# Decays of a state-space mixer: products with a 0/1 tile against loads from a DRAM tile with a maximum on VectorE

## The chip, the cores and the metric

The kernel runs on one core of one Trainium2 chip. The metric is the device time in microseconds (us) of one execution. TensorE (PE in the rows) multiplies, VectorE (DVE) and ScalarE (ACT) work elementwise, GpSimd (POOL) does small elementwise work, and SyncE (SP) starts nearly all loads. Every engine takes its own instructions strictly in the order in which they were written for it, so an instruction that waits holds up all that stand behind it on that engine.

## What is computed

One layer of a hybrid decoder: two token mixers, their merge, an MLP, a gated embedding and norms, for 512 tokens of 1024 channels. The change lies in one of the mixers, Mamba-2 SSD, in the factor `l_dec`:

```
def ssd_mixer(z, xbc, dt_raw, w_conv, b_conv, dt_bias, a_log, d_skip, out_norm):
    ...                                   # G=4 groups, J=8 heads each, P=64, N=128, chunks of L=128, nc=4
    dt = jax.nn.softplus(dt_raw.astype(f32) + dt_bias.astype(f32))
    a_head = -jnp.exp(a_log.astype(f32)).reshape(G, J)
    ...
    a_cs = jnp.cumsum(dtc * a_head, axis=2)
    Xdt = X * dtc[..., None]
    seg = a_cs[:, :, :, None] - a_cs[:, :, None]
    causal = jnp.tril(jnp.ones((L, L), dtype=bool))[:, :, None, None]
    l_dec = jnp.exp(jnp.where(causal, seg, -jnp.inf))
    scores = jnp.einsum('bclgn,bcsgn->bclsg', Cc, Bc)
    y_diag = jnp.einsum('bclsgj,bcsgjp->bclgjp', scores[..., None] * l_dec, Xdt)
    ...
```

For each of 32 heads and 4 chunks `l_dec` is a 128 x 128 matrix: `exp(a_cs[l] - a_cs[s])` for l >= s. Position s lies on the partitions, l along the free axis, so the row `a_cs[l]` of a head has to be spread over all 128 partitions first. The kernel holds `-a_cs` (it grows along a chunk, and is never negative).

## The kernel before

Products of fp32 matrices are made of three products of rounded parts (a high part and a rest): `mm3`, or the like in `proj_b`. Weights come by SP into two `raw` buffers (line 154), ScalarE rounds them to `whi` (line 164), VectorE makes the rest `wlo` (line 165), each in four buffers, and TensorE takes both (lines 169 to 171 for `proj_a` with results `pa`, 249 to 251 for `proj_b` with results `pb`). The results lie in four PSUM buffers `mm`; small results (`yd`, `yo`, `st`, `bc`, `ot`, ...) lie in four others, `sm`.

The SSD mixer goes group by group. For a group g: `ssd_proj` makes x, B and C by products with the input, with a convolution of four taps on VectorE (`acc`, line 549) and transposes; `ssd_z` makes the gate `sz`; `ssd_pre` makes the scores `scm` and the decays L; `ssd_core` goes over the four chunks, `ssd_gate` gates, normalizes and transposes (`ot`), and `ssd_branch` multiplies with the output weights of the group before. In `ssd_core` a chunk c takes: L times `scm` on VectorE (line 615), `xdt` (617), eight small products `yd` (624), the state's product `yo` for c > 0 (621), the state's update `st` (632) with `S` on VectorE (641), and additions to `Xg` (647, 651) and the gate (660). The product `yo` of chunk c + 1 needs `S` of chunk c.

The decays of a group come in `ssd_pre`: the `-a_cs` of all heads lies as two rounded parts in rows 0 to 63 of the tile `ncsT`, and rows 64 to 127 hold 2^100 at the triangle's forbidden places. A 0/1 tile `sel` picks a head's two rows (GpSimd writes it anew for each group, line 591) and adds the forbidden rows to it: two products a head, one for each half of the 128 positions, spread the sum over the partitions in PSUM (`bc`, line 600), and four `exp` on ScalarE (line 602), one a chunk, write L from it with the own `a_cs[s]` as bias `qt`. There are four L buffers, one a chunk.

Before this, once, a block works out `dt` and `-a_cs` (the tile `dt_s`, named s2) for all heads on VectorE and ScalarE with rows of 32 partitions, and transposes four such rows of results, collected in `dt_Q`, by the product `psq` to `qt`.

The order on each engine comes from a scheduler that simulates the timeline while the program is built; code blocks can be moved ahead in its priorities (`ahead`). So a change in one place moves instructions in others too.

Of the kernel before, what the change touches and what calls it, by code (L numbers as in the profile page):

```python
# [23 lines left out]
HPG = 8  # L24
# [14 lines left out]
def f32(ap):  # L39
    return ap.bitcast(F32)  # L40
# [3 lines left out]
def tile_hybrid_block(  # L44
# [21 lines left out]
    nc = tc.nc  # L66
    V, S, G, TE = nc.vector, nc.scalar, nc.gpsimd, nc.tensor

    cp = ctx.enter_context(tc.tile_pool(name="cp", bufs=1))
# [11 lines left out]
    def sm_ps(name):  # L81
        return psm.tile([P, T], F32, tag="sm", name=name, bufs=4)


    ident = cp.tile([P, P], F32, name="ident")
# [7 lines left out]
        out=cmask, in_=cmask, pattern=[[1, P]], compare_op=ALU.is_ge, fill=0.0,  # L93
# [7 lines left out]
        base=0, channel_multiplier=-1,  # L101
    )
    G.memset(gmask[:64, 64:], 0.0)
    sel64 = cp.tile([64, 32], R, name="sel64")
    V.tensor_copy(sel64[0:32, :], ident[0:32, 0:32])
    V.tensor_copy(sel64[32:64, :], ident[32:64, 32:64])
    prm = cp.tile([P, 232], F32, name="prm")
    dsk = cp.tile([P, 32], F32, name="dsk")

# [384 lines left out]
    wgt = dts.tile([48, 512], F32, name="wgt")  # L494
    nc.sync.dma_start(wgt[32:48, :], w_gla_gate)
    qt = dts.tile([P, NT, P], F32, name="qt")
    ncsT = dts.tile([P, T], R, name="ncsT")
    cdb = dts.tile([P, NT, 32], F32, name="cdb")


    sx = ExitStack()
    sp = sx.enter_context(tc.tile_pool(name="sp", bufs=1, reuse_waits="tile"))

    sel = sp.tile([P, 2, HPG, P], R, name="sel")
    if True:
        pick = sp.tile([P, 2, P], F32, tag="S", name="pick", bufs=2)
        G.memset(pick, 0.0)  # L510
        for v in range(2):

            G.affine_select(
                out=pick[:, v, :], in_=pick[:, v, :], pattern=[[1, P]], compare_op=ALU.not_equal, fill=1.0,
                base=64 - 64 * v, channel_multiplier=-1,
            )

        G.memset(pick[64:65, 0, :64], 0.0)
        G.memset(pick[64:65, 0, 64:], 1.0)
        G.memset(pick[64:65, 1, :], 0.0)  # L520
        G.tensor_copy(sel[64:], pick[64:].unsqueeze(2).to_broadcast([64, 2, HPG, P]))


    def heads(ap, c0, g):

# [50 lines left out]
    def ssd_pre(g):  # L576
        Xg, BT, CT = st[g]["X"], st[g]["BT"], st[g]["CT"]
        ps = sm_ps(f"bt{g}")
        for c in range(NT):
            TE.transpose(ps[:, c * P : (c + 1) * P], BT[:, c * P : (c + 1) * P], ident)  # L580
        Bt = sp.tile([P, NT, P], F32, tag="Bt", name=f"Btok{g}", bufs=1)
        S.copy(Bt, ps.rearrange("p (c n) -> p c n", c=NT))
        ps = sm_ps(f"sc{g}")
        for c in range(NT):
            cc = slice(c * P, (c + 1) * P)
            TE.matmul(ps[:, cc], lhsT=BT[:, cc], rhs=CT[:, cc], start=True, stop=True)
        sc = sp.tile([P, NT, P], F32, tag="sc", name=f"scm{g}", bufs=1)
        V.tensor_tensor(
            sc, ps.rearrange("p (c l) -> p c l", c=NT), cmask.unsqueeze(1).to_broadcast([P, NT, P]), op=ALU.mult
        )  # L590
        G.tensor_copy(
            sel[:64], sel64[:, 8 * g : 8 * g + 8].unsqueeze(1).unsqueeze(3).to_broadcast([64, 2, HPG, P])
        )
        Ls = [sp.tile([P, HPG, P], F32, tag="L", name=f"L{g}_{c}", bufs=4) for c in range(NT)]
        for j in range(HPG):
            h = 8 * g + j
            pb = sm_ps(f"bc{h}").rearrange("p (c v l) -> p c v l", c=NT, v=2)
            nv = ncsT.rearrange("p (c v l) -> p c v l", c=NT, v=2)
            for v in range(2):
                TE.matmul(pb[:, :, v, :], lhsT=sel[:, v, j, :], rhs=nv[:, :, v, :], start=True, stop=True)  # L600
            for c in range(NT):
                S.activation(
                    Ls[c][:, j, :].rearrange("p (v l) -> p v l", v=2), pb[:, c], AF.Exp, scale=-1.0,
                    bias=qt[:, c, 32 + h : 33 + h],
                )
        st[g].update(Bt=Bt, Ls=Ls, sc=sc)

# [87 lines left out]
    if True:  # L695
# [9 lines left out]
        def tl(tag, name, rows=32):  # L705
# [5 lines left out]
        smask = tl("S", "smask")  # L711
        G.memset(smask, 1.0)
        G.memset(smask.rearrange("p (c l) -> p c l", c=NT)[:, :, 0:1], 0.0)

        far = sp.tile([P, 64], F32, tag="S", name="far", bufs=2)
        G.memset(far, 2.0**100)
        G.affine_select(
            out=far, in_=far, pattern=[[-1, 64]], compare_op=ALU.is_ge, fill=0.0, base=-65, channel_multiplier=1,
        )
        G.memset(far[64:65, :], 2.0**100)  # L720
        G.tensor_copy(
            ncsT[64:, :].rearrange("p (c l) -> p c l", l=64), far[64:, :].unsqueeze(1).to_broadcast([64, 8, 64])
        )
        ae = cp.tile([32, 1], F32, name="ae")
        S.activation(ae, alog, AF.Exp)
        V.tensor_scalar(out=xr, in0=ps[:32, :], scalar1=dtb, scalar2=None, op0=ALU.add)
# [17 lines left out]
        V.tensor_scalar(out=s1, in0=xr, scalar1=ae, scalar2=None, op0=ALU.mult)  # L744
        V.tensor_tensor_scan(out=s2, data0=smask, data1=s1, initial=0.0, op0=ALU.mult, op1=ALU.add)
        S.copy(Q[32:64, :], s2)
        S.copy(ncsT[0:32, :], s2)
        V.tensor_tensor(ab, s2, f32(ncsT[0:32, :]), op=ALU.subtract)
        S.copy(ncsT[32:64, :], ab)
        S.activation(Q[64:96, :], s2, AF.Exp, scale=-1.0)  # L750
        s2v = s2.rearrange("p (c l) -> p c l", c=NT)
        V.tensor_tensor(
# [488 lines left out]
```

## Time and profile before

| | us |
|---|---|
| median of 3 runs | 1181.87 |
| lowest, highest | 1176.79, 1185.32 |
| the profiled execution, its own time | 1176.31 |
| its span, first to last instruction | 1174.6 |
| TensorE busy | 1152.0 |
| VectorE busy | 684.4 |
| ScalarE busy | 519.6 |
| GpSimd busy | 154.7 |

Times in the rows are us from the start of the span. The SSD mixer takes the stretch up to about 390 us. Busy time of TensorE counts matmuls that overlap: the time from one start to the next is what one costs. "Idle before" is what an engine sat without work before an instruction, and the name after the arrow is what it waited for. The SP queue's own rows show the transfers it starts, not their landing.

### The profile page before, as it was taken

The page shows a single profiled execution, that of the slowest core. Times are in us where ns is not written, and L with a number is a line of the kernel's source. Part 1 is how long each engine was busy: PE and PEld are TensorE (multiplying, and loading weights), DVE is VectorE, ACT ScalarE, POOL GpSimd, SP SyncE. Part 2 cuts the span into 40 slices and gives each one's busy share as a digit, 9 for nine tenths or more (in the row PEclk, how much of TensorE's full clock was granted, in tenths as well). Part 3 has the DMA queues.
Part 4 walks back from the last instruction along what each step waited for, and adds up shares of the span by engine and source line. Part 5 has one row for each costly group of instructions (what it writes and reads, how often), then busy time and mean ns, then how long its engine had stood idle before and what let it go on. Part 6 is the DMA issues. An engine that isn't in the chain of part 4 may idle for free.

```text
span 1174.6 us, 14039 instructions
## 1 busy us (share of the span) xinstructions
PE 1152.0 (98%) x5540; PEld 955.2 (81%) x5540; DVE 684.4 (58%) x901; ACT 519.6 (44%) x846; POOL 154.7 (13%) x142
## 2 busy tenths in 40 slices
PE   6999999999999999999999999999999999999997
PEld 5887887888887678888888888898888888888786
DVE  6766747767557547244234334665566755766865
ACT  4566483572482217442433232444334443344553
POOL 6003114032013000000021110000021000201212
PEclk9999999999999999999999999999999999999999
DMA  7332122222322143322224332743426452445221
GB/s 209 108 90 79 48 73 72 72 74 72 107 72 74 36 136 119 104 72 72 72 72 126 82 98 72 204 138 95 121 72 177 116 161 84 114 132 122 90 90 72
DMA packets 150177, 117.39 MB, mean 100 GB/s; under 512 B 5456, under 2 KB 124880, under 8 KB 150112
## 3 DMA queue, kind: packets, MB, share of 16 engines
q1 hardware_dynamic: 146048, 107.59, 31.5%
q0 software_dynamic: 2912, 5.77, 2.9%
q10 hardware_dynamic: 1152, 3.15, 0.7%
q8 instruction: 43, 0.70, 0.3%
q14 instruction: 22, 0.18, 0.0%
HBM read 114.40 MB, written 2.10 MB: 99 GB/s over the span
## 4 chain that ended last, share of the span: by engine, by line
PE 94%; DVE 2%; ACT 1%; DMA 1%; issue 1%; SPq 1%; POOL 0%; POOLq 0%; ACTq 0%; DVEq 0%
PE pa L170 18%; PE pa L169 18%; PE pa L171 18%; PE pb L249 7%; PE pb L250 7%; PE pb L251 7%; PE yd L624 2%; PE sX L349 2%; PE sX L348 2%; PE sX L350 2%; PE st L632 1%; PE yo L621 1%; PE sZ L349 1%; PE sZ L350 1%; PE sZ L348 1%; DMA raw<-in_w_in_dram 1%
## 5 line engine op out<-in xcount | busy, mean ns | idle before, releaser
L165 DVE TENSOR_TENSOR wlo<-raw,whi 128x1024 fp32r<-128x1024 f32 (+1 forms) x208 | 261.1, 1262 | 253.4 <-ACT whi L164 253.1
L164 ACT CAST whi<-raw 128x1024 fp32r<-128x1024 f32 (+1 forms) x209 | 216.5, 1039 | 356.5 <-PE pa L170 225.1
L169 PE MATMUL pa<-h1h,whi 128*128 128x512 f32 (+1 forms) x416 | 160.0, 385 | 0.5 <-ACT h1h L419 0.4
L171 PE MATMUL pa<-h1h,wlo 128*128 128x512 f32 (+1 forms) x416 | 157.6, 379 | 0.0
L170 PE MATMUL pa<-h1l,whi 128*128 128x512 f32 (+1 forms) x416 | 156.8, 377 | 0.1
L170 PE MATMUL pa<-h2l,whi 128*128 128x512 f32 (+1 forms) x384 | 142.7, 372 | 0.0
L169 PE MATMUL pa<-h2h,whi 128*128 128x512 f32 (+1 forms) x384 | 142.4, 372 | 0.0
L171 PE MATMUL pa<-h2h,wlo 128*128 128x512 f32 (+1 forms) x384 | 142.2, 372 | 0.0
L249 PE MATMUL pb<-whi,h1h 128*128 128x512 f32 x256 | 99.8, 394 | 0.8 <-DVE accb L684 0.8
L250 PE MATMUL pb<-wlo,h1h 128*128 128x512 f32 x256 | 99.9, 390 | 0.0
L251 PE MATMUL pb<-whi,h1l 128*128 128x512 f32 x256 | 99.5, 392 | 0.0
L169 PEld LDWEIGHTS pa<-h1h,whi 128*128 128x128 f32 x416 | 79.5, 191 | 15.2 <-ACT h1h L419 0.8
L170 PEld LDWEIGHTS pa<-h1l,whi 128*128 128x128 f32 x416 | 79.4, 191 | 14.3 <-issue 0.7
L171 PEld LDWEIGHTS pa<-h1h,wlo 128*128 128x128 f32 x416 | 79.2, 190 | 13.8 <-issue 0.2
L170 PEld LDWEIGHTS pa<-h2l,whi 128*128 128x128 f32 x384 | 72.4, 189 | 12.5
L171 PEld LDWEIGHTS pa<-h2h,wlo 128*128 128x128 f32 x384 | 72.3, 189 | 12.3
L169 PEld LDWEIGHTS pa<-h2h,whi 128*128 128x128 f32 x384 | 72.2, 189 | 12.4
L249 PEld LDWEIGHTS pb<-whi,h1h 128*128 128x128 f32 x256 | 48.1, 188 | 10.5 <-DVE accb L684 1.2
L251 PEld LDWEIGHTS pb<-whi,h1l 128*128 128x128 f32 x256 | 48.1, 188 | 9.7
L250 PEld LDWEIGHTS pb<-wlo,h1h 128*128 128x128 f32 x256 | 48.1, 188 | 9.3
L549 DVE SCALAR_TENSOR_TENSOR acc<-pa,prm,acc 128x511 f32<-128x511 f32 (+2 forms) x72 | 52.6, 742 | 2.9 <-ACT acc L547 2.0
L170 PE MATMUL pa<-obl,whi 128*128 128x512 f32 x128 | 52.0, 406 | 0.0
(380 smaller groups left out, 1981.7 us busy)
## 6 DMA issues: line engine op xcount, KB each, us to landing
raw<-in_w_in_dram SPq DMA_DIRECT2D x48, 512.0 KB, 5.1
raw<-in_w_ffn_up_dram SPq DMA_DIRECT2D x44, 512.0 KB, 5.2
raw<-in_w_in_dram SPq DMA_DIRECT2D x16, 1024.0 KB, 5.1
raw<-in_w_ffn_down_dram SPq DMA_DIRECT2D x10, 1024.0 KB, 5.3
raw<-in_w_branch_b_dram SPq DMA_DIRECT2D x32, 256.0 KB, 3.8
raw<-in_w_branch_a_dram SPq DMA_DIRECT2D x8, 512.0 KB, 4.8
raw<-in_w_out_dram SPq DMA_DIRECT2D x4, 1024.0 KB, 4.9
raw<-in_w_ffn_down_dram POOLq DMA_DIRECT2D x4, 1024.0 KB, 8.7
```

What stands on the lines that cost most here:

```text
L164: S.copy(hi, raw)
L165: eng.tensor_tensor(lo, raw, f32(hi), op=ALU.subtract)
L169: TE.matmul(ps, lhsT=lh, rhs=rh, start=first, stop=False)
L170: TE.matmul(ps, lhsT=lh, rhs=rl, start=False, stop=False)
L171: TE.matmul(ps, lhsT=ll, rhs=rh, start=False, stop=last)
L249: TE.matmul(pss[t], lhsT=a, rhs=hi[:, kk, :], start=first, stop=False)
L250: TE.matmul(pss[t], lhsT=a, rhs=lo[:, kk, :], start=False, stop=False)
L251: TE.matmul(pss[t], lhsT=b, rhs=hi[:, kk, :], start=False, stop=last)
L348: TE.matmul(ps, lhsT=a_h, rhs=hi[:, k % 2, :], start=new and k == 0, stop=False, skip_group_check=True)
L349: TE.matmul(ps, lhsT=a_h, rhs=lo[:, k % 2, :], start=False, stop=False, skip_group_check=True)
L350: TE.matmul(ps, lhsT=a_l, rhs=hi[:, k % 2, :], start=False, stop=k == kh - 1, skip_group_check=True)
L549: V.scalar_tensor_tensor(out=acc[:, s:], in0=ps[:, : T - s], scalar=cw[:, ct, 3 - s : 4 - s], in1=acc[:, s:], op0=ALU.mult, op1=ALU.add,)
```

## The change

The products `bc`, the tiles `sel`, `sel64`, `pick`, `far` and `ncsT` and all that fills them are gone. In their place `-a_cs` is written to a tile in DRAM, `ncsd`, by four transfers from ScalarE's queue, one a chunk. For each group and chunk SP loads the 8 heads' rows (8 x 128 numbers, 4 KB in one piece) into all 128 partitions of the L buffer. VectorE replaces each value by the maximum of it and the own value of the partition (so that forbidden places get exp(0) = 1, which `scm` then zeroes), and the `exp` of ScalarE works in place, eight a chunk, now chunk by chunk.

```diff
-    sel64 = cp.tile([64, 32], R, name="sel64")
-    V.tensor_copy(sel64[0:32, :], ident[0:32, 0:32])
-    V.tensor_copy(sel64[32:64, :], ident[32:64, 32:64])
...
-    ncsT = dts.tile([P, T], R, name="ncsT")
+
+    dram = ctx.enter_context(tc.tile_pool(name="dram", bufs=1, space=bass.MemoryType.DRAM))
+    ncsd = dram.tile([NT, 32, P], F32, name="ncsd")
...
-    sel = sp.tile([P, 2, HPG, P], R, name="sel")
...
-        G.tensor_copy(sel[64:], pick[64:].unsqueeze(2).to_broadcast([64, 2, HPG, P]))
...
-        G.tensor_copy(
-            sel[:64], sel64[:, 8 * g : 8 * g + 8].unsqueeze(1).unsqueeze(3).to_broadcast([64, 2, HPG, P])
-        )
+
         Ls = [sp.tile([P, HPG, P], F32, tag="L", name=f"L{g}_{c}", bufs=4) for c in range(NT)]
-        for j in range(HPG):
-            h = 8 * g + j
-            pb = sm_ps(f"bc{h}").rearrange("p (c v l) -> p c v l", c=NT, v=2)
-            nv = ncsT.rearrange("p (c v l) -> p c v l", c=NT, v=2)
-            for v in range(2):
-                TE.matmul(pb[:, :, v, :], lhsT=sel[:, v, j, :], rhs=nv[:, :, v, :], start=True, stop=True)
-            for c in range(NT):
+        for c in range(NT):
+            src = ncsd[c : c + 1, 8 * g : 8 * g + 8, :].rearrange("c h l -> c (h l)").to_broadcast([P, HPG * P])
+            nc.sync.dma_start(Ls[c].rearrange("p h l -> p (h l)"), src)
+            own = qt[:, c, 32 + 8 * g : 40 + 8 * g].unsqueeze(2).to_broadcast([P, HPG, P])
+            V.tensor_tensor(Ls[c], Ls[c], own, op=ALU.max)
+            for j in range(HPG):
+                h = 8 * g + j
                 S.activation(
-                    Ls[c][:, j, :].rearrange("p (v l) -> p v l", v=2), pb[:, c], AF.Exp, scale=-1.0,
-                    bias=qt[:, c, 32 + h : 33 + h],
+                    Ls[c][:, j, :], Ls[c][:, j, :], AF.Exp, scale=-1.0, bias=qt[:, c, 32 + h : 33 + h],
                 )
...
-        S.copy(ncsT[0:32, :], s2)
-        V.tensor_tensor(ab, s2, f32(ncsT[0:32, :]), op=ALU.subtract)
-        S.copy(ncsT[32:64, :], ab)
+        for c in range(NT):
+            nc.scalar.dma_start(ncsd[c], s2[:, c * P : (c + 1) * P])
```

The order moves with it. SP, while group 1 is in `ssd_core`: the names `raw` are weights (of group 2's input products and gate), `L_0` to `L_3` the decays of the next group. Before:

```order
L154 DMA raw_1762<-in_w_in_dram 128x8x128 [waits DMAHW6_49,DMAHW1_49,DMAHW7_49,DMAHW0_49,DVE_49]
L154 DMA raw_1762<-in_w_in_dram 128x8x128
L154 DMA raw_1968<-in_w_in_dram 128x8x128 [waits DMAHW3_49,DMAHW2_49,DVE_49]
L154 DMA raw_1968<-in_w_in_dram 128x8x128
L154 DMA raw_2152<-in_w_in_dram 128x4x512 [waits DMAHW5_49,DMAHW4_49,DVE_49]
L154 DMA raw_2162<-in_w_in_dram 128x4x512 [waits DMAHW7_49,DMAHW6_49,DVE_49]
```

With the change, SP at the same place:

```order
L151 DMA raw_1899<-in_w_in_dram 128x8x128 [waits DMAHW7_49,DMAHW6_49,DVE_49]
L151 DMA raw_1899<-in_w_in_dram 128x8x128
L574 DMA L_0_1855<-ncsd 128x1024 [waits PE_49]
L574 DMA L_1_1856<-ncsd 128x1024 [waits DMAHW5_49,PE_49]
L574 DMA L_2_1857<-ncsd 128x1024 [waits PE_49]
L151 DMA raw_2083<-in_w_in_dram 128x4x512 [waits DMAHW1_49,DMAHW0_49,DVE_49]
L574 DMA L_3_1858<-ncsd 128x1024 [waits PE_49]
L151 DMA raw_2093<-in_w_in_dram 128x4x512 [waits DMAHW3_49,DMAHW2_49,DVE_49]
```

SP now waits for TensorE too: a load of L takes the buffer that the `yd` products of the same chunk, one group earlier, have read, and three such loads stand ahead of the gate's weights.

VectorE in the same stretch, from the first chunk's `yd` of group 1 to the update of the state. Before:

```order
L647 TENSOR_TENSOR Xg_962<-Xg_962,yd_0_1332 128x512
L617 TENSOR_TENSOR xdt_2_1376<-Xg_962,qt 128x512
L660 TENSOR_TENSOR Xg_962<-Xg_962,sz_0_1420 128x512
L650 TENSOR_TENSOR yt_1_1372<-yo_1_1352,qt 128x512
L165 TENSOR_TENSOR wlo_1807<-raw_1762,whi_1806 128x1024
L647 TENSOR_TENSOR Xg_962<-Xg_962,yd_1_1354 128x512
L617 TENSOR_TENSOR xdt_3_1402<-Xg_962,qt 128x512
L651 TENSOR_TENSOR Xg_962<-Xg_962,yt_1_1372 128x512
L641 TENSOR_TENSOR S_1_1367<-S_1_1367,st_1_1365 128x512
```

With the change, VectorE from the same instruction on:

```order
L623 TENSOR_TENSOR Xg_927<-Xg_927,yd_0_1280 128x512
L593 TENSOR_TENSOR xdt_2_1324<-Xg_927,qt 128x512
L636 TENSOR_TENSOR Xg_927<-Xg_927,sz_0_1368 128x512
L576 TENSOR_TENSOR L_0_1855<-L_0_1855,qt 128x1024
L162 TENSOR_TENSOR wlo_1714<-raw_1710,whi_1713 128x1024
L626 TENSOR_TENSOR yt_1_1320<-yo_1_1300,qt 128x512
L623 TENSOR_TENSOR Xg_927<-Xg_927,yd_1_1302 128x512
L593 TENSOR_TENSOR xdt_3_1350<-Xg_927,qt 128x512
L627 TENSOR_TENSOR Xg_927<-Xg_927,yt_1_1320 128x512
L617 TENSOR_TENSOR S_1_1315<-S_1_1315,st_1_1313 128x512
```

The maximum of group 2's first chunk stands three instructions behind the addition of the `yd` that frees its buffer, and the weights' rests, the additions and the state's update stand behind it. It is so for all four chunks, and for the groups 0 to 2 alike.

ScalarE in the block that works out `-a_cs` (`dt_s_532` before and `dt_s_518` now is s2), up to the first gate `sz_0`. Before:

```order
L746 COPY dt_Q<-dt_s_532 32x512
L747 CAST ncsT<-dt_s_532 32x512
L750 ACT_TABLE_LOAD
L750 ACTIVATE dt_Q<-dt_s_532 32x512
L756 ACTIVATE dt_s_531<-dt_s_531 32x512
L164 CAST whi_1003<-raw_965 128x1024
L749 CAST ncsT<-dt_ab 32x512
L758 COPY dt_Q<-dt_q 32x512
L164 CAST whi_1041<-raw_1038 128x1024
L573 ACT_TABLE_LOAD
L573 ACTIVATE sz_0_834<-pb_838 128x512
```

With the change, ScalarE:

```order
L712 COPY dt_Q<-dt_s_518 32x512
L714 DMA ncsd<-dt_s_518 32x128 x3
L161 CAST whi_968<-raw_930 128x1024
L714 DMA ncsd<-dt_s_518 32x128
L715 ACT_TABLE_LOAD
L715 ACTIVATE dt_Q<-dt_s_518 32x512
L721 ACTIVATE dt_s_517<-dt_s_517 32x512
L161 CAST whi_1006<-raw_1003 128x1024
L723 COPY dt_Q<-dt_q 32x512
L552 ACT_TABLE_LOAD
L552 ACTIVATE sz_0_799<-pb_803 128x512
```

Two casts to `ncsT` are gone, four starts of transfers have come, and a weight's rounding (`whi_1041` before, `whi_1006` now) stands ahead of the last copy to `dt_Q`.

## Rows read from the trace of the kernel before

**Rows 1.** The page: TensorE's busy time in the span, and the chain that ended last.

```profile
PE 1152.0 (98%) x5540; PEld 955.2 (81%) x5540; DVE 684.4 (58%) x901; ACT 519.6 (44%) x846; POOL 154.7 (13%) x142
...
PE 94%; DVE 2%; ACT 1%; DMA 1%; issue 1%; SPq 1%; POOL 0%; POOLq 0%; ACTq 0%; DVEq 0%
```

**Rows 2.** The tile view of bc: ns min/median/max, first and last start, shape.

```profile
L600 PEld LDWEIGHTS bc<-ncsT,sel x64: 187/188/193, 88.7 to 344.1; 128*128 128x128 f32 x64
L600 PE MATMUL bc<-ncsT,sel x64: 274/281/365, 88.7 to 344.2; 128*128 128x256 f32 x64
```

**Rows 3.** TensorE's timeline in group 0's decays: start us, length us.

```profile
93.23 0.40 PE L600 MATMUL bc<-ncsT,sel 128*128 128x256 f32 x2
93.47 0.39 PE L170 MATMUL pa<-h1l,whi 128*128 128x512 f32 x1
```

**Rows 4.** TensorE's timeline at the first chunk of group 0, idle time in brackets.

```profile
110.13 1.97 PE L624 MATMUL yd<-xdt,L 128*128 128x64 f32 x16 [1.58 <-DVE xdt L617]
...
113.69 0.70 PE L621 MATMUL yo<-S,CT 128*128 128x512 f32 x1 [0.68 <-ACT S L635]
```

**Rows 5.** ScalarE's timeline: ten of the exp in one run.

```profile
94.18 2.69 ACT L602 ACTIVATE L<-bc,qt 128x128 f32<-128x128 f32 x10
```

**Rows 6.** ScalarE's timeline at the block of -a_cs, and a later transfer start.

```profile
77.62 0.62 ACT L749 CAST ncsT<-dt_ab 32x512 fp32r<-32x512 f32 x1
78.27 0.62 ACT L758 COPY dt_Q<-dt_q 32x512 f32<-32x512 f32 x1
...
81.28 1.09 ACT L573 ACTIVATE sz<-pb 128x512 f32<-128x512 f32 x2
...
1159.27 0.37 ACTq L1176 DMA_DIRECT2D out_dram<-on  x1
```

**Rows 7.** DMA issues: KB each, median us from issue to landing.

```profile
out_dram<-on ACTq DMA_DIRECT2D x4, 256.0 KB, 2.8
...
g<-in_mixer_norm_dram SPq DMA_DIRECT2D x1, 512.0 KB, 5.0
...
g<-in_final_norm_dram SPq DMA_DIRECT2D x1, 512.0 KB, 3.5
```

**Rows 8.** VectorE's groups between 60 and 390 us: busy us, mean ns, idle before.

```profile
L615 DVE TENSOR_TENSOR L<-L,scm 128x1024 f32<-128x1024 f32 x16 | 25.5, 1653 | 2.5 <-ACT L L602 2.4
L660 DVE TENSOR_TENSOR Xg<-Xg,sz 128x512 f32<-128x512 f32 x16 | 15.1, 941 | 0.1
...
L617 DVE TENSOR_TENSOR xdt<-Xg,qt 128x512 f32<-128x512 f32 x16 | 11.9, 761 | 0.0
L647 DVE TENSOR_TENSOR Xg<-Xg,yd 128x512 f32<-128x512 f32 x16 | 10.9, 682 | 3.5 <-PE yd L624 3.4
```

**Rows 9.** Stretches: length, busy us of PE, PEld, DVE, ACT, POOL; clock; DMA share, GB/s.

```profile
60.00:100.00 40.00, 39.95 (x193) 33.38 (x192) 21.45 (x28) 27.57 (x53) 0.00 (x0) 1.00 0.29 80
100.00:140.00 40.00, 37.74 (x195) 29.99 (x195) 34.15 (x43) 18.28 (x33) 13.69 (x10) 1.00 0.26 79
140.00:180.00 40.00, 40.00 (x202) 33.51 (x201) 20.62 (x25) 29.40 (x62) 6.58 (x5) 1.00 0.20 54
180.00:220.00 40.00, 39.95 (x198) 32.22 (x198) 29.47 (x38) 14.46 (x24) 12.32 (x9) 1.00 0.27 79
...
260.00:300.00 40.00, 40.00 (x195) 32.09 (x195) 27.75 (x37) 9.74 (x17) 10.16 (x8) 1.00 0.27 73
```

**Rows 10.** The timeline: a weight's rest on VectorE, and its first product.

```profile
132.82 1.22 DVE L165 TENSOR_TENSOR wlo<-raw,whi 128x1024 fp32r<-128x1024 f32 x1 [2.76 <-ACT whi L164]
...
143.44 0.39 PE L249 MATMUL pb<-whi,h1h 128*128 128x512 f32 x1
```

**Rows 11.** The timeline: start of the gate's weights of group 2, and their first product.

```profile
190.96 17.84 SPq L154 DMA_DIRECT2D raw<-in_w_in_dram  x2
...
232.56 0.39 PE L249 MATMUL pb<-whi,h1h 128*128 128x512 f32 x1
```

**Rows 12.** The chain: the third chunk's yd of group 1, start us and length.

```profile
198.55 1.73 PE yd L624 x16
```

More of the change, by code (lines that the diff above doesn't have):

```diff
@@ L502, in tile_hybrid_block @@
     sp = sx.enter_context(tc.tile_pool(name="sp", bufs=1, reuse_waits="tile"))
-    sel = sp.tile([P, 2, HPG, P], R, name="sel")
-    if True:
-        pick = sp.tile([P, 2, P], F32, tag="S", name="pick", bufs=2)
-        G.memset(pick, 0.0)
-        for v in range(2):
-            G.affine_select(
-                out=pick[:, v, :], in_=pick[:, v, :], pattern=[[1, P]], compare_op=ALU.not_equal, fill=1.0,
-                base=64 - 64 * v, channel_multiplier=-1,
-            )
-        G.memset(pick[64:65, 0, :64], 0.0)
-        G.memset(pick[64:65, 0, 64:], 1.0)
-        G.memset(pick[64:65, 1, :], 0.0)
-        G.tensor_copy(sel[64:], pick[64:].unsqueeze(2).to_broadcast([64, 2, HPG, P]))
     def heads(ap, c0, g):
@@ L590, in ssd_pre @@
         )
-        G.tensor_copy(
-            sel[:64], sel64[:, 8 * g : 8 * g + 8].unsqueeze(1).unsqueeze(3).to_broadcast([64, 2, HPG, P])
-        )
         Ls = [sp.tile([P, HPG, P], F32, tag="L", name=f"L{g}_{c}", bufs=4) for c in range(NT)]
-        for j in range(HPG):
-            h = 8 * g + j
-            pb = sm_ps(f"bc{h}").rearrange("p (c v l) -> p c v l", c=NT, v=2)
-            nv = ncsT.rearrange("p (c v l) -> p c v l", c=NT, v=2)
-            for v in range(2):
-                TE.matmul(pb[:, :, v, :], lhsT=sel[:, v, j, :], rhs=nv[:, :, v, :], start=True, stop=True)
-            for c in range(NT):
+        for c in range(NT):
[5 more added lines that the diff above has]
+                h = 8 * g + j
                 S.activation(
-                    Ls[c][:, j, :].rearrange("p (v l) -> p v l", v=2), pb[:, c], AF.Exp, scale=-1.0,
-                    bias=qt[:, c, 32 + h : 33 + h],
+                    Ls[c][:, j, :], Ls[c][:, j, :], AF.Exp, scale=-1.0, bias=qt[:, c, 32 + h : 33 + h],
                 )
@@ L713, in tile_hybrid_block @@
         G.memset(smask.rearrange("p (c l) -> p c l", c=NT)[:, :, 0:1], 0.0)
[L715 to L723, printed above, removed]
         ae = cp.tile([32, 1], F32, name="ae")
```

## The prediction

> **What bounds the kernel now.** I read the page first: TensorE is busy 98% of the span and carries 94% of the chain that ended last; VectorE carries 2% [rows 1]. So two things can move the time: TensorE work that goes away or comes, and TensorE standing idle. Then the tile view of `bc` for the size of the work that goes [rows 2], and TensorE's timeline around it for what one pair costs in its stream [rows 3]. In the timeline of the first chunk the reader is to see the idle time in brackets: 1.58 us ahead of the first `yd`, and 0.68 us ahead of a `yo` [rows 4]. The stretches say where VectorE, the engine that gets the new work, has room: it is busy 34.15 of 40 us from 100 on, 29.47 from 180 on, 27.75 from 260 on, but 21.45 from 60 on and 20.62 from 140 on [rows 9]. TensorE fills 37.7 to 40 us of each at a granted clock of 1.00, its upper level (2.4 GHz), so the products' price needs no correction for the clock.
>
> **The products go.** 64 matmuls of `bc`, in 32 pairs [rows 2]. Their duration of 281 ns each would give 64 x 0.281 = 18.0 us, but that counts overlap. The pair at 93.23 is followed by the next product at 93.47 [rows 3]: about 0.235 us a pair (I allow for the rounding), 32 x 0.235 = 7.5 us. Nothing takes their place on TensorE, and they lie in a stream with hardly a gap, so the whole 7.5 us is taken as path: **-7.5**.
>
> The weight loads of `bc` are 64 of 188 ns, 12.0 us [rows 2]. A pair's spacing of 0.235 us is less than two such loads (0.376), so here the loads do not set the pace. The Trainium skill ("Perfetto Trace Analysis", section "Identifying the Most-Contended Engine") holds matmul busy time for a poor measure, because matmuls are pipelined, and judges TensorE by the busy share of its weight loads. About the busy time the row agrees with it (18.0 against 7.5 us); by the second half 12.0 us would be freed in place of 7.5, which is rival 3.
>
> **The first wait.** The 1.58 us at 110 ended with `xdt` on VectorE [rows 4], which was late because `L` times `scm` had stood waiting for the exps (2.4 us of waits, all for ScalarE) [rows 8]. Before, the exps go head by head over all chunks, so the first chunk is complete only with the last of the group's eight heads; now eight exps finish a chunk. Ten exps take 2.69 us [rows 5], so a chunk takes 2.1, and its load has some 25 us from the block of `-a_cs` (77.62 to 78.27 [rows 6]) to the first use. So the wait goes: **-1.6** (bounds 0 and -1.6). What is late next is the `yo` behind it, which waits for `S` by ScalarE; its 0.68 us are kept, and if they go the sum falls by 0.7.
>
> **The block of -a_cs on ScalarE.** Two casts of 0.62 us go, one of them at 77.62; four starts of transfers come. A start takes 0.37 us on this queue [rows 6], rounded up to 0.5 at most: 1.5 to 2.0 us against 1.2, so +0.3 to +0.8 of ScalarE before `sz` at 81.28. That `sz` empties a PSUM buffer for TensorE; the block's last copy at 78.27 ends 2.4 us earlier than `sz` starts, which covers most of it if TensorE's products and not the copy set the start of `sz`. I take **+0.4**, with 0 (covered) and +2.0 (nothing covered, the whole of the starts) as bounds. `wlo`, `whi` and the transposes behind are as before.
>
> **The maxima on VectorE.** No row shows a 128x1024 maximum with one operand repeated. Nearest below is `wlo`, a subtraction of 128x1024 in 1.22 us [rows 10]; nearest above the product `L` times `scm` of the same tile, 1653 ns in the mean [rows 8]. I take 1.4, since both are one pass over 1024 elements and the upper one is a mean with a repeated operand like this one. For group 0 the four (5.6 us) fall into the stretch from 60 on, 21.45 + 5.6 = 27 of 40 us [rows 9]: nothing. Each exp also moves from a PSUM source to an L buffer in place, as many as before; I leave their price unchanged.
>
> For groups 1 to 3 the maximum brings a wait with it. Its load needs the buffer that the `yd` of the same chunk one group earlier reads, so it starts when that `yd` ends, and on VectorE only the three steps behind that `yd` stand ahead of the maximum: 0.68 + 0.76 + 0.94 = 2.4 us [rows 8]. A load of 512 KB landed after 3.5 and 5.0 us, both of them one row spread over all partitions, and 256 KB after 2.8 [rows 7]. So VectorE stands at the maximum for 1.1 to 2.6 us, middle 1.9, and behind it in the queue are the rest of a weight, the other additions, the state `S` (for the next `yo`) and the gate. With the maximum itself: 1.4 + 1.9 = 3.3 us a chunk (bounds 2.3 and 4.25), four times in each stage that has a group's core: 13.2 us (9.3 and 17.0).
>
> That is weighed in the three stages where it falls [rows 9]: 34.15 + 13.2 = 47.4, over 40 by 7.4; 29.47 + 13.2 = 42.7, over by 2.7; 27.75 + 13.2 = 41.0, over by 1.0. Together 11.1 us of VectorE's work that doesn't fit its stage. Part of it is absorbed: `wlo` at 132.82 is done 9.4 us before its first product at 143.44 [rows 10], and the stretch behind, from 140 on, has 19 us of room. What has no such lead is `S`, the convolution that empties a PSUM buffer and the gate, and TensorE's waits at this place are already for VectorE and `S` [rows 4]. I take two thirds as reaching TensorE, an estimate: **+7.4**. Bounds: 9.3 a stage gives an overrun of 3.4 us, in the first alone, and none of it may pass: 0. 17.0 a stage gives 11.2 + 6.5 + 4.8 = 22.4 us, all of it passing.
>
> The Trainium skill ("DMA: Bandwidth & Descriptors", section "Anatomy of one DMA — SWDGE (gpsimd) path") puts a transfer at about 2.0 us fixed and its bytes at 436 GB/s; for 512 KB I work out an estimate of 3.2 us by it. Both 512 KB rows lie above. By 3.2 a wait would be 0.8 us and a stage 4 x 2.2 = 8.8 us, over by 2.95 us in the first stage alone; two thirds of it pass, and the sum would be -6.7.
>
> **Covered.** SP's queue: the gate's weights, started at 190.96 before, now stand behind the load of `L_2`, which waits for the third chunk's `yd` to end at 198.55 + 1.73 = 200.3 [rows 11, 12]. 9.3 us late, against 41.6 us up to their first product at 232.56 [rows 11]; 32 us remain for landing, rounding and the rest: zero, and 9.3 if the cover were gone. Transfers: four loads a stage are 2.1 MB in 40 us, 52 GB/s on top of 73 to 79 at a share of 0.26 to 0.27 [rows 9]; in proportion the share goes to about 0.45: zero. ScalarE: eight exps (2.1 us) now stand in its queue until the maximum is done, with squares and roundings behind; it is busy 14.46 of 40 in the stage from 180 on, 18.28 from 100 on: zero, and their delay is in the upper bound of VectorE. GpSimd loses its copies to `sel` (13.69 us of busy time in the first stage holds them); nothing on the chain waits for it [rows 1].
>
> **The sum.** Against the profiled execution's 1176.31: -7.5 - 1.6 + 0.4 + 7.4 = -1.3, so 1175.0. The median of the runs shown, 1181.87, is 0.47% above the profiled one; scaled, 1180.6. That is 0.1% under before. One per cent, about 12 us, is what a measurement of this kernel can tell from no change, since its three runs lie 8.5 us apart. So the forecast is no change.
>
> **Rival 1: the cover holds.** The landing is near 3.5 us or the lead of weights and accumulators takes up the overrun. For it: `wlo` lies 9.4 us ahead, and the neighbouring stretches have half of VectorE free [rows 9, 10]. Against: `S` and the gate have no lead. Then -7.5 - 1.6 + 0.4 = -8.7, and with the `yo` wait half gone -9.0: 1167.3, scaled 1172.8. 0.8% faster. Chance 0.22.
>
> **Rival 2: the queue behind the maximum becomes the bound (slower).** One mechanism: VectorE stands for a load at each of the 12 maxima of groups 1 to 3, with `S`, the convolution and the gate behind it, and TensorE waits for these. With landings of 5.0 us and maxima of 1.65 us the overrun is 22.4 us: -8.7 + 22.4 = +13.7, 1190.0, scaled 1195.6, 1.2% slower. It decides from 8.7 us that pass through (slower than before) and from 20.5 (slower by 1%). Landings beyond 5 us, when a load meets weights on the queues, would take it further. For it: VectorE is at 85% in the first of these stages [rows 9], and its wait is for something that starts only when TensorE is done. Against: an overrun spreads into the next stretch, with 19 us of room. Chance 0.18.
>
> **Rival 3: a weight load sets the price of a product.** Then 12.0 us go in place of 7.5, and the sum is -5.8: 1170.5, scaled 1176.0, 0.5% faster. Against it speaks the pair's spacing [rows 3]. That rule is the one of the Trainium skill's "Perfetto Trace Analysis" named above. Chance 0.05.
>
> **How the numbers follow.** Forecast 0.55, rivals 0.22, 0.18 and 0.05. The range: from 1169 (rival 1 with all of the 0.68 us gone, about 1172, and 0.3% for the runs' scatter) to 1195 (rival 2's own figure, with its further part left out). Faster by over 1% means under 1170.0: only the lower tail of rivals 1 and 3, 0.08. Slower by over 1% means above 1193.7: most of rival 2 and a little of the forecast's tail, 0.14. Within 1%: 0.78.
>
> **What will show it.** Products: no `bc` rows, and TensorE's stream between 88 and 100 without the 0.235 us steps. First wait: no idle time ahead of the first `yd`. Maxima: their mean duration between 1.22 and 1.65 us, and idle time ahead of them put down to a DMA, 1.1 to 2.6 us at each of 12; loads of L landing in 3.5 to 5.0 us. Overrun: new idle time on TensorE ahead of `yo`, `pa`, `pb` or `ot` in groups 1 and 2, released by VectorE, some 7 us in all. Block: `sz` at most 2 us later against the products around it. I am wrong if the loads land much later than 5 us (then rival 2), if TensorE shows no new idle time (rival 1), or if the sum is off through something that these rows don't show, such as weights that come late behind a blocked SP queue.

## The result and the profile after

| | before | changed |
|---|---|---|
| median, us | 1179.33 (4 runs) | 1168.52 (4 runs) |
| lowest to highest, us | 1176.44 to 1185.32 | 1167.36 to 1169.18 |
| ratio, 95% interval | 1 | 0.9899, 0.9866 to 0.9931 |
| the profiled execution, us | 1176.31 | 1167.36 |

The change takes off 10.8 us, 1.0% (9.0 us between the two profiled executions). The slower runs of the kernel before have a lower mean granted clock (beside the experiments 1174.8 us of span at 0.999 and 1181.0 at 0.992), so the traces below explain the 9.0. The forecast was 1180.6, no change, with a range from 1169.0: the time lies just under the range and on the side of rival 1, which gave 1172.8.

The page of the changed kernel, against [rows 1]:

```profile
PE 1143.2 (98%) x5476; PEld 947.1 (81%) x5476; DVE 698.4 (60%) x914; ACT 529.8 (45%) x850; POOL 143.4 (12%) x127
```

VectorE has 14 us more to do and TensorE 64 products less. The view of waits, all that TensorE waited for between 40 and 430 us (the mixer and what leads into the next block), kernel before, then changed kernel (engine and line, what it waited for: us in total, times, longest):

```profile
PE yd L624 <- DVE xdt L617: 1.6, 1, 1.6
PE yo L621 <- ACT S L635: 0.7, 1, 0.7
PE pa L169 <- ACT obh L672: 0.5, 1, 0.5
PE ot L670 <- DVE Xg L664: 0.2, 1, 0.2
```

```profile
PE pb L246 <- DVE accb L660: 0.8, 1, 0.8
```

Both waits of [rows 4] are gone, and two more at the last group's `ot` (0.2 us ahead of it, 0.5 behind it): 3.0 us in all. The one for `accb` stands in the kernel before as well, just behind this window. There is no new one in the SSD mixer. VectorE does stand at the maxima, as forecast. The tile view of L, changed kernel (SP's loads, then the maximum, ns min/median/max; what VectorE's maxima waited for; the landing):

```profile
L574 SPq DMA_DIRECT2D L<-ncsd x16: 320/340/3781, 73.3 to 271.3; - x16
L576 DVE TENSOR_TENSOR L<-L,qt x16: 1212/1222/2059, 83.8 to 275.9; 128x1024 f32<-128x1024 f32 x16
...
DMA L<-ncsd: 17.2, 5
...
DMA to landing us min/median/max: 3.3/4.6/8.7
```

Most maxima take 1.22 us, the lower bound of [rows 10], and two 2.06: 1.33 in the mean (21.0 us of VectorE's busy time for 16), not far from the 1.4 taken. The waits are 17.2 us at 5 of 12 maxima, up to 6.0, not 1.9 at each. VectorE's longest waits from 60 to 400 us, kernel before, then changed kernel:

```profile
DVE wlo L165 <- ACT whi L164: 76.0, 30, 9.2
```

```profile
DVE wlo L162 <- ACT whi L161: 27.8, 26, 4.3
DVE L L576 <- DMA L<-ncsd: 17.2, 5, 6.0
```

The kernel before already let VectorE wait 76 us here, for a rounding that itself mostly waits for products (53.0 us of ScalarE's waits ahead of `whi`). The changed kernel puts maxima and loads into part of that idle time. Not all of the fall to 27.8 is their doing: without loads and maxima it is 52.9 (experiments). VectorE's busy time in the stretches, against [rows 9] and one more line of the kernel before, which stands first:

```profile
220.00:260.00 40.00, 40.00 (x212) 33.87 (x211) 25.44 (x27) 30.95 (x62) 6.79 (x5) 1.00 0.29 79
```

```profile
60.00:100.00 40.00, 40.00 (x191) 33.42 (x190) 31.85 (x38) 31.84 (x61) 2.32 (x2) 1.00 0.46 134
100.00:140.00 40.00, 40.00 (x203) 32.34 (x203) 33.87 (x41) 26.00 (x51) 10.94 (x8) 1.00 0.42 132
140.00:180.00 40.00, 40.00 (x207) 33.15 (x206) 29.17 (x31) 27.38 (x49) 11.38 (x9) 1.00 0.37 97
180.00:220.00 40.00, 40.00 (x191) 32.66 (x190) 28.88 (x38) 24.98 (x51) 4.08 (x4) 1.00 0.31 104
220.00:260.00 40.00, 40.00 (x207) 32.83 (x206) 30.46 (x33) 21.38 (x37) 12.71 (x9) 1.00 0.31 91
```

The full stretch from 100 on stays at 34. The stretches that had room take the work: 60 to 100 most of all (21.45 to 31.85, with group 0's maxima and other work that comes earlier), then 140 to 180 (20.62 to 29.17) and 220 to 260 (25.44 to 30.46). TensorE is busy throughout. The transfers' share is 0.42 in place of 0.26 from 100 on, near the 0.45 worked out, and 0.31 to 0.37 from 140 on.

Going back from TensorE's timeline: the first product `gg` of the next block starts at 392.91 before and 380.75 in the changed kernel, 12.2 us earlier. By the first product `sX` (870.67 and 860.75) it is 9.9. So 2.2 us are given back in between, although TensorE's order is the same in both kernels there; 1.9 of them at two products, changed kernel:

```profile
453.45 0.50 PE L246 MATMUL pb<-whi,h1h 128*128 128x512 f32 x1 [0.70 <-DVE E L813]
...
455.85 0.50 PE L246 MATMUL pb<-whi,h1h 128*128 128x512 f32 x1 [0.75 <-DVE E L818]
```

This is the gate of the second mixer, which the change doesn't touch. On ScalarE the four `exp` and four `ln` of that gate came in another order; its timeline, changed kernel, a part:

```profile
432.01 1.28 ACT L783 ACT_TABLE_LOAD   x1
433.30 0.63 ACT L783 ACTIVATE ge<-ge 128x512 f32<-128x512 f32 x1
433.95 1.28 ACT L779 ACT_TABLE_LOAD   x1
435.25 0.64 ACT L779 ACTIVATE ge<-ge 128x512 f32<-128x512 f32 x1
```

Here each turn from one function to the other loads a table, 1.28 us: nine loads in this block, five in the kernel before.

### The profile page after: what moved, and what is told of

Read it like the earlier page. It is cut to its first block, busy times and chain, and to the rows that moved or that the text cites. A ratio compares the mean times of both kernels' runs of the same rounds, so it can differ in the third digit from the quotient of the medians.

```text
span 1165.3 us, 13943 instructions
## 1 busy us (share of the span) xinstructions
PE 1143.2 (98%) x5476; PEld 947.1 (81%) x5476; DVE 698.4 (60%) x914; ACT 529.8 (45%) x850; POOL 143.4 (12%) x127
## 3 DMA queue, kind: packets, MB, share of 16 engines
q1 hardware_dynamic: 148352, 115.98, 34.4%
## 4 chain that ended last, share of the span: by engine, by line
PE 92%; DVE 2%; ACT 2%; DMA 1%; SPq 1%; issue 1%; POOL 0%; POOLq 0%; ACTq 0%; DVEq 0%
PE pa L167 17%; PE pa L168 17%; PE pa L166 17%; PE pb L246 7%; PE pb L248 7%; PE pb L247 7%; PE yd L600 2%; PE sX L345 2%; PE sX L346 2%; PE sX L347 2%; DMA raw<-in_w_in_dram 1%; PE st L608 1%; PE yo L597 1%; PE sZ L347 1%; PE sZ L345 1%; PE sZ L346 1%
```

## Experiments

Times are medians; the ratio to the kernel before, with its interval, is from runs on the same chip. A small edit also moves instructions that it doesn't name, since the order comes from a simulated timeline, so each reading rests on the run's own waits as well.

**The products put back.**

```diff
+        for j in range(HPG):
+            pb = sm_ps(f"bc{8 * g + j}")
+            for v in range(2):
+                TE.matmul(
+                    pb[:, 256 * v : 256 * v + 256], lhsT=hT[0][:, 0, :P], rhs=hT[0][:, 0, 0:256], start=True, stop=True
+                )
         for c in range(NT):
```

> The changed kernel with 64 products of 128x128 by 128x256 put back, two for each head at the place where the decays are made, into results that nobody reads. Cover theory (TensorE's stream alone sets the time, and one pair costs its spacing of 0.235 to 0.246 us): 7.5 to 7.9 us above the changed kernel's 1168.5, so about 1176, with no idle time of TensorE that is new. Weight-load theory: 12 us above, about 1180.5. Order theory (the gain came from another order and waits that went, not from the products): under 2 us above, about 1170.

Measured 1177.77, ratio 0.9981 (0.9967 to 0.9996): 9.3 us above the changed kernel. From each start to the next, the 64 products take 7.8 us of TensorE's stream, in a trace whose `bc` rows look like [rows 2]:

```profile
L575 PEld LDWEIGHTS bc<-h1h x64: 187/188/193, 88.5 to 339.8; 128*128 128x128 f32 x64
L575 PE MATMUL bc<-h1h x64: 275/283/365, 88.6 to 339.9; 128*128 128x256 f32 x64
```

The 12 us of their weight loads aren't paid. Another 0.9 us is at two places near 157 us, where the next product starts after 0.56 and 0.74 us in place of the usual 0.23, with waits of 0.18 us for `obh` and 0.35 for `obl`: a little new idle time, which the expectation had ruled out. From 42 us, the first product of the block of `-a_cs`, to `gg` the whole difference is 9.4. The waits of [rows 4] do not come back.

**The kernel before without its products,** and nothing in their place (the decays are a constant function of a 0/1 tile here, not those of the reference).

```diff
         for j in range(HPG):
-            h = 8 * g + j
...
-            for v in range(2):
-                TE.matmul(pb[:, :, v, :], lhsT=sel[:, v, j, :], rhs=nv[:, :, v, :], start=True, stop=True)
             for c in range(NT):
-                S.activation(
-                    Ls[c][:, j, :].rearrange("p (v l) -> p v l", v=2), pb[:, c], AF.Exp, scale=-1.0,
-                    bias=qt[:, c, 32 + h : 33 + h],
-                )
+                S.activation(Ls[c][:, j, :], cmask, AF.Exp, scale=-1.0, bias=neghalf[:, 0:1])
```

> The kernel before without its 64 products bc, and nothing in their place: the exps, still head by head, read the causal 0/1 tile with a constant bias (so the decays are not those of the reference); no loads of L, no maxima. Product theory: the 7.9 us of spacing go, and with them part of the waits at group 0's first chunk, since the exps no longer wait for TensorE: 8 to 11.5 us under the kernel before, that is within 3 us of the changed kernel's 1168.5. Order theory (the gain is the changed kernel's own order and its chunks): under 5 us below the kernel before.

Measured 1166.69, ratio 0.9902 (0.9884 to 0.9921), 11.7 us under the kernel before, 0.2 beyond the expected range: the changed kernel's gain without its loads, maxima or order. The waits ahead of the first `yd` and at the last `ot` are gone here too; 0.8 us ahead of a `yo` stayed. The product theory holds, the order theory falls. One thing goes beyond the products: exps of a constant wait for their buffers alone, and group 0's begin at 24.7 us.

**The changed kernel without loads and maxima** (decays constant as above).

```diff
...
-            nc.sync.dma_start(Ls[c].rearrange("p h l -> p (h l)"), src)
...
-            V.tensor_tensor(Ls[c], Ls[c], own, op=ALU.max)
...
-                    Ls[c][:, j, :], Ls[c][:, j, :], AF.Exp, scale=-1.0, bias=qt[:, c, 32 + h : 33 + h],
+                    Ls[c][:, j, :], cmask, AF.Exp, scale=-1.0, bias=neghalf[:, 0:1],
```

> The changed kernel without the 16 loads of L and without the 16 maxima; the exps read the causal 0/1 tile with a constant bias, so the decays are not those of the reference. It prices all that the change added on SP, the transfers and VectorE. Cover theory: the added work costs nothing, within 1.5 us of 1168.5. Overrun theory: 5 us and more under 1168.5.

Measured 1169.49, ratio 0.9908 (0.9878 to 0.9937), 1.0 above the changed kernel; from the block of `-a_cs` to `gg` it takes 339.7 us, the changed kernel 338.5. Sixteen loads of 512 KB and 21 us of VectorE cost nothing that can be measured. Here too the exps wait for their buffers alone. VectorE's longest waits from 60 to 400 us:

```profile
DVE wlo L162 <- ACT whi L161: 52.9, 31, 6.0
```

So of the 48.2 us by which the changed kernel shortens these waits, 25.1 go with the loads and maxima; the rest went without them.

**Six buffers for L,** so that two loads a group don't wait.

```diff
-        Ls = [sp.tile([P, HPG, P], F32, tag="L", name=f"L{g}_{c}", bufs=4) for c in range(NT)]
+        Ls = [sp.tile([P, HPG, P], F32, tag="L", name=f"L{g}_{c}", bufs=6) for c in range(NT)]
```

> The changed kernel with six buffers for L in place of four, so that the loads of two chunks of the next group need not wait for this group's yd. Cover theory (VectorE's 17 us of waits for loads cost nothing): VectorE's waits fall to about half, the time stays within 1.5 us of 1168.5. Overrun theory: 4 us and more under 1168.5.

Measured 1170.85, ratio 0.9916 (0.9888 to 0.9945), 2.3 above the changed kernel, where the cover theory allowed 1.5. VectorE's waits for L fell to 9.2 us (2 times), as expected, while the new order brought TensorE two waits (1.9 and 1.5 us) and spared it those near 453. Taking 8 us of VectorE's waiting away won nothing, which speaks against the overrun theory; but with an order that changed so much the run alone doesn't show that the waits were free.

**Every load twice,** into the same buffer, to make VectorE wait longer. It ran twice (the second label speaks of three loads; it is this kernel with two).

```diff
             nc.sync.dma_start(Ls[c].rearrange("p h l -> p (h l)"), src)
+            nc.sync.dma_start(Ls[c].rearrange("p h l -> p (h l)"), src)
```

> The changed kernel with every load of L done twice into the same buffer, the second behind the first, so that the landing that VectorE waits for comes 3 to 5 us later. Cover theory: VectorE's waits at the maxima grow from 17 us to 30 us and more, TensorE still shows at most 2 us of new idle time, time within 3 us of 1168.5. Overrun theory (two thirds of what VectorE loses reaches TensorE, as was forecast): 10 us and more above 1168.5.

> A second look at the kernel that loads every L twice, one profile, for its scatter: TensorE's wait for S ahead of a yo near 181 us again, 2 to 3 us by the lead theory (a VectorE wait of 6.8 us is longer than the 2 to 3 us that S is ahead of its product plus the 4.2 us that the changed kernel waits there); no wait there by the cover theory in its plain form.

Measured 1170.88, ratio 0.9933 (0.991 to 0.9956), and 1171.08: about 2.5 above the changed kernel. VectorE waited 26.6 and 27.1 us, less than the 30 expected, and now some of it came through: TensorE waited 2.2 us for `S` in the first run and 1.8 in the second. VectorE's and TensorE's timelines of the first run:

```profile
178.55 1.23 DVE L577 TENSOR_TENSOR L<-L,qt 128x1024 f32<-128x1024 f32 x1 [6.80 <-DMA L<-ncsd]
179.69 0.68 DVE L624 TENSOR_TENSOR Xg<-Xg,yd 128x512 f32<-128x512 f32 x1
180.29 0.69 DVE L594 TENSOR_TENSOR xdt<-Xg,qt 128x512 f32<-128x512 f32 x1
180.89 0.68 DVE L618 TENSOR_TENSOR S<-S,st 128x512 f32<-128x512 f32 x1
```

```profile
169.34 1.02 PE L598 MATMUL yo<-S,CT 128*128 128x512 f32 x2
...
181.63 1.13 PE L598 MATMUL yo<-S,CT 128*128 128x512 f32 x2 [2.23 <-DVE S L618]
```

That is the chain of rival 2: the maximum holds up `S`, and `yo` waits for it. In the changed kernel the same chain has a lead, VectorE's and TensorE's timelines there:

```profile
176.68 1.23 DVE L576 TENSOR_TENSOR L<-L,qt 128x1024 f32<-128x1024 f32 x1 [4.20 <-DMA L<-ncsd]
...
181.36 0.68 DVE L617 TENSOR_TENSOR S<-S,st 128x512 f32<-128x512 f32 x1
...
251.22 1.23 DVE L576 TENSOR_TENSOR L<-L,qt 128x1024 f32<-128x1024 f32 x1 [6.00 <-DMA L<-ncsd]
...
256.50 0.68 DVE L617 TENSOR_TENSOR S<-S,st 128x512 f32<-128x512 f32 x1
```

```profile
175.43 1.02 PE L597 MATMUL yo<-S,CT 128*128 128x512 f32 x2
...
185.10 1.02 PE L597 MATMUL yo<-S,CT 128*128 128x512 f32 x2
...
259.28 1.02 PE L597 MATMUL yo<-S,CT 128*128 128x512 f32 x2
```

`S` is done at 182.04 and 257.18, 3.1 and 2.1 us ahead of its product, although VectorE had stood for 4.2 and 6.0 us. Counted from the group's first `yo`, `S` is done after 6.6 us in the changed kernel (175.43 to 182.04) and after 12.2 with two loads (169.34 to 181.57). Of these 5.6 us the lead took 3.1, and the 2.2 of the wait are most of the rest. Not all of the delay is the longer wait: TensorE's and VectorE's order also changed, and the maximum comes later against the products. So the plain cover theory is too broad: a delay of `S` is free only up to its lead.

**Every load three times,** one more line of the same kind.

> The changed kernel with each load of L done three times into the same buffer. Lead theory (the state S is 2 to 3 us ahead of its product in the changed kernel, and a wait of TensorE of over 2 us is followed by some 7 us at half the granted clock): TensorE waits for S ahead of several yo, 2 us and more each, and the time is 6 to 25 us above the changed kernel's 1168.5. Cover theory in its plain form (VectorE's waits cost nothing): within 3 us of the runs with two loads, 1171.

Measured 1187.89, ratio 1.0085 (1.0064 to 1.0106): 19.4 us above the changed kernel (20.4 above its runs on the same chip) and slower than before. VectorE waited 34.4 us for L. TensorE's waits there:

```profile
PE xt L540 <- ACT acc L537: 5.7, 2, 3.3
PE pb L246 <- ACT sz L552: 5.6, 1, 5.6
PE yo L599 <- DVE S L619: 1.4, 2, 1.3
```

ScalarE's and VectorE's timelines ahead of the wait of 5.6 us:

```profile
145.78 2.45 ACT L581 ACTIVATE L<-L,qt 128x128 f32<-128x128 f32 x8 [5.30 <-DVE L L578]
...
149.54 0.60 ACT L552 ACTIVATE sz<-pb 128x512 f32<-128x512 f32 x1
```

```profile
144.52 1.23 DVE L578 TENSOR_TENSOR L<-L,qt 128x1024 f32<-128x1024 f32 x1 [4.42 <-DMA L<-ncsd]
```

Twice the changed kernel's wait turns the gain into a loss. Most of it came by another way than expected, and only 1.4 us are waits for `S`. The gate's `sz` stands on ScalarE behind exps that wait for the late maximum. The two `acc` (3.3 and 2.4 us) come behind VectorE's convolution; ahead of the first a maximum had waited 1.7 us, but what made them late was not followed up. The waits are 12.7 us; behind the three long ones the granted clock is 0.50, 0.73 and 0.72 over the next 6 us, which by an estimate from these shares adds some 6 us.

**Exps head by head.** In the changed kernel the loops over heads and chunks were exchanged.

```diff
-            for j in range(HPG):
-                h = 8 * g + j
+        for j in range(HPG):
+            h = 8 * g + j
+            for c in range(NT):
                 S.activation(
                     Ls[c][:, j, :], Ls[c][:, j, :], AF.Exp, scale=-1.0, bias=qt[:, c, 32 + h : 33 + h],
                 )
```

> The changed kernel with the exps again head by head over the four chunks, behind all four maxima of a group. If the two waits of TensorE at group 0's first chunk (1.58 us ahead of yd, 0.68 us ahead of yo) went because exps now finish a chunk at a time: they come back, 1.5 to 2.7 us above the changed kernel's 1168.5. If they went because the loads are there long before the products would be: nothing comes back, within 1 us.

Measured 1168.98, ratio 0.9914 (0.9892 to 0.9937), and inconclusive: the first two chunks' maxima are done first, so their 16 exps ran first all the same. The order was then forced for group 0 by a bias that depends on the last maximum:

```diff
-            for j in range(HPG):
+            for j in range(HPG if g > 0 else 0):
...
+        if g == 0:
+            qb = cp.tile([P, NT, HPG], F32, name="qb")
+            V.scalar_tensor_tensor(
+                out=qb, in0=Ls[3][:, :, 0].unsqueeze(1).to_broadcast([P, NT, HPG]), scalar=0.0,
+                in1=qt[:, :, 32:40], op0=ALU.mult, op1=ALU.add,
+            )
+            for j in range(HPG):
+                for c in range(NT):
+                    S.activation(Ls[c][:, j, :], Ls[c][:, j, :], AF.Exp, scale=-1.0, bias=qb[:, c, j : j + 1])
```

> The changed kernel with the 32 exps of group 0 alone held until all four maxima are done and taken head by head over the chunks (one more small VectorE instruction of 128x32 makes their bias from the last maximum). This forces the order that the earlier run by head did not get. If finishing a chunk at a time is why TensorE's 1.58 us ahead of the first yd and 0.68 us ahead of the first yo went: they come back, 1.5 to 2.5 us above the changed kernel's 1168.5. If they went because the exps start about 5 us earlier (85.1 us against 90.4): under 0.7 us above.

Measured 1173.53, ratio 0.996 (0.9942 to 0.9978), 5.0 above the changed kernel, but not for the reason asked after: the exps started at 90.59 and ran head by head, and neither the first `yd` nor a `yo` waited. TensorE waited at another place:

```profile
145.04 0.79 PE L246 MATMUL pb<-whi,h1h 128*128 128x512 f32 x1 [3.73 <-ACT sz L552]
```

ScalarE had stood 5.07 us for a maximum that itself had waited 4.58 us for its load, with `sz` behind the exps, as with three loads.

**The Ln behind all Exp** in the second mixer's gate (the block that the expectation means), changed kernel.

```diff
+    one = gp.tile([P, 1], F32, name="one")
+    G.tensor_scalar(out=one, in0=gtmp[3][:, 0:1], scalar1=0.0, scalar2=1.0, op0=ALU.mult, op1=ALU.add)
     for h in range(GH):
         bc, e = bcum[h], gtmp[h]
-        S.activation(e, e, AF.Ln, bias=1.0)
+        S.activation(e, e, AF.Ln, bias=one)
```

> The changed kernel with the four Ln of the gate block behind the MLP's start of the second mixer held until all four Exp of it are done (their bias of 1 is worked out from the last Exp's tile), so that ScalarE changes its function table fewer times between 429 and 447 us. If the 2.3 us that the changed kernel loses against the kernel before between 418 and 460 us come from these table loads (nine against five): 2 to 2.5 us under 1168.5, about 1166.2, and no idle time ahead of the products of line 246 near 453 and 456. If they come from something else (late weights): no change.

> The changed kernel as it is, on the chip and beside the runs of the next one: 1167 to 1169.5 us by its four runs so far.

> The changed kernel with the Ln held behind the four Exp once more, beside the changed kernel itself: 2 to 3.5 us under it if the earlier difference (1165.4 against 1168.5, in different calls) holds; within 1 us of it if that was the chip.

Measured 1165.37, ratio 0.9882 (0.9863 to 0.9902), and again 1166.84, 0.99 (0.9878 to 0.9921), beside 1167.49, 0.9912 (0.9894 to 0.993), for the changed kernel on the same chip. Three table loads are left of nine, and in both runs the waits near 453 are gone. Every run with nine loads in this block has these waits, and none with five or three, six buffers and the kernel before without products among them; so they do come from the table loads. By medians the gain is 3.1 and 0.7 us, the second within the 1 us that the last expectation put down to the chip. In the traces the stretch from `gg` to `sX` is 2.2 us shorter in the first run (477.8 for 480.0) and the lowest times of the second pair lie 2.1 apart (1165.35, 1167.43); its profiled execution lost 1.4 us elsewhere (last section). It has the lowest medians of the kernels that compute the reference.

## Why the prediction was wrong

**The products: right.** -7.5 was forecast. Summed from each start to the next the 64 products of the kernel before took 7.9 us, and 7.8 when put back. Rival 3's 12.0 us, and with it the rule of the Trainium skill ("Perfetto Trace Analysis", section "Identifying the Most-Contended Engine") as I had used it for a price, falls: the weight loads overlapped.

**The maxima on VectorE: the step that failed.** "What has no such lead is `S`, the convolution that empties a PSUM buffer and the gate [...] I take two thirds as reaching TensorE": +7.4; measured 0. The size of a maximum was near (1.33 us for 1.4); two other things were off. The stages of 40 us were treated as closed, while work moved into the ones beside them and into time that VectorE had spent waiting for `whi`. And `S` does have a lead. VectorE's and TensorE's timelines, kernel before:

```profile
202.25 0.68 DVE L641 TENSOR_TENSOR S<-S,st 128x512 f32<-128x512 f32 x1
```

```profile
207.43 1.02 PE L621 MATMUL yo<-S,CT 128*128 128x512 f32 x2
```

`S` ends at 202.93, 4.5 us ahead of its `yo`, with other products in between. Over all 12 `yo` of the kernel before the lead is 3.7 to 4.5 us, but for the one of [rows 4], which has none; I had read that one and taken it for all. In the changed kernel it is 2.1 to 4.3: the maxima and their waits took at most some 2 us of it, so nothing reached TensorE. Without loads and maxima the time is the same. With two loads the lead is used up at one `yo`, and 2.2 us come through: the mechanism of rival 2, with another point of decision. A lead per chunk decides, not a sum per stage. With three loads the +7.4 and more are there, but only 1.4 us by `S`; the longest wait, 5.6 us, came by ScalarE's exps, whose delay the prediction had put at zero outside VectorE's bound.

**The first wait: right in size, its reason shown in part.** -1.6 was forecast and the wait went. Finishing a chunk at a time isn't needed for that: with the order of the kernel before forced on group 0's exps the wait stayed away too. Nor is it the products in TensorE's stream: put back, they leave as many products ahead of the first `yd` as before, 138 from `psq` on, and there is no wait. What is gone in every run without the wait is that the exps wait for the products' results; in the kernel before, four L times `scm` on VectorE wait for these exps, and the first `xdt` stands behind them (109.31). In the run without products `xdt` keeps that place and the exps are earlier; in the run with the forced order the exps are as late as before and `xdt` stands ahead of L times `scm` (98.91). Which of the two does it in the changed kernel stays open, since each edit also moved what TensorE does ahead of `yd`. The `yo` wait, kept in the sum, and 0.7 us at the last `ot` went as well: 1.4 us that the forecast left out.

**The block of -a_cs: wrong in sign, and small.** +0.4 was taken. `sz` starts at 80.13 in place of 81.28: the starts of transfers overlapped ScalarE's copies, and the two casts were no longer ahead of it. TensorE's products there moved by less than 0.2 us.

**Covered: right for the changed kernel.** TensorE waited for no late weight in the SSD mixer, and the transfers' share came out near what was worked out. The exps behind a late maximum, taken as zero, cost nothing here either, but with three loads they brought the longest wait. Landing times were wider than [rows 7]: 8.7 us at most. The loads of the first chunks stand right behind a pair of weights on SP, and there VectorE waited 4.2 and 6.0 us. The 3.2 us worked out from the Trainium skill ("DMA: Bandwidth & Descriptors", section "Anatomy of one DMA — SWDGE (gpsimd) path") is just under the shortest landing, 3.3, and 1.4 under the median; that figure is for transfers that GpSimd starts, and these are started by SP.

**Not foreseen: the give-back.** 2.2 us at the second mixer's gate, from four more table loads. The prediction looked at the order inside the SSD mixer alone; behind it TensorE's is the same in both kernels, ScalarE's is not.

**The scaling: too large.** All sums were raised by 0.47%, since the median of three runs of the kernel before lay so far above its profiled execution. Its medians in the runs since are 1178.1 to 1179.3, 0.15 to 0.26% above, and the changed kernel's is 0.1% above its own. The bottom of the range, 1169.0, rests on this step: rival 1's sum without it, 1167.3, is the measured 1167.36 of the profiled execution. That is partly luck, since its terms (-7.5, -1.6, +0.4, -0.3) were measured as -7.9 and -4.3, with 2.8 given back behind the mixer.

The sum as measured, up to `gg`: -7.9 for products, -3.0 for waits, and -1.3 in small shifts between other products that were not followed up, together -12.2; then +2.2, and 0.6 at the end: -9.3 of span.

## What to carry to other kernels

Price a product that goes by the distance from its start to the next one. Price work that comes to another engine by the lead of what stands behind it: for each dependent product the time from its operand's end to its start, over all instances, not over the one that waits; here a lead of some 4 us a chunk, with idle time of VectorE ahead of it, swallowed waits of up to 6 us. Do the same for every engine that the late work releases: twice the waiting cost 19 us, and its longest wait came by ScalarE, whose exps stood ahead of a gate. Where a scheduler sets the order, compare the order of every engine to the end of the program: an untouched block gave back a fifth of the gain.

## What the hardware showed beside

A wait of TensorE can cost more than its length. In the run with group 0's exps by head, the stretches around the 3.73 us wait (length, busy us of PE, PEld, DVE, ACT, POOL; granted clock; DMA):

```profile
130.00:141.00 11.00, 11.00 (x61) 9.07 (x59) 4.23 (x6) 4.07 (x14) 0.00 (x0) 1.00 0.55 176
141.00:145.00 4.00, 0.32 (x2) 0.00 (x0) 3.03 (x5) 3.97 (x7) 0.00 (x0) 0.91 0.11 43
145.00:151.00 6.00, 5.96 (x14) 4.70 (x15) 3.94 (x6) 5.46 (x14) 0.00 (x0) 0.50 0.01 3
151.00:155.00 4.00, 4.00 (x18) 3.26 (x18) 1.68 (x4) 2.33 (x3) 1.21 (x2) 0.99 0.00 0
```

For 6 us behind the wait the granted clock is 0.50, the lower of the two levels (1.2 GHz), and only 14 products go through. So the wait of 3.7 costs about 3 us more. Behind the 2.23 us wait of the run with two loads the clock was 0.61 over 6.4 us; behind a wait of 1.87 us (six buffers) and the 1.58 us of [rows 4] it stayed at 1.00.

The same happens without a wait. In the second run with the Ln held back, some 9 us behind the first of the `gg` products (of 16 rows), the clock is at half, and in the first run of the same kernel not:

```profile
390.00:393.40 3.40, 3.40 (x9) 2.64 (x10) 0.69 (x1) 0.00 (x0) 0.00 (x0) 0.53 0.71 211
```

```profile
390.00:393.40 3.40, 3.40 (x16) 2.76 (x16) 1.43 (x3) 1.05 (x1) 0.00 (x0) 1.00 0.55 192
```

Nine products against 16: 1.4 us of difference between two executions of one program, the size of the scatter between its runs (1165.3 to 1166.9). Six of the 14 profiled executions have this stretch, with products put back, without loads and maxima, and with three loads among them; from the first `gg` to the first product `att` they take 1.3 to 1.8 us more than those with as many table loads and without it. So a difference of under 2 us between two medians here says nothing by itself. What decides it was not tried.
